# The last output projection of an RWKV layer: operands loaded ahead, the last window results split in place, and the next stage's first weights in turn with it

## The chip, the cores and the metric

The kernel runs on one core of a Trainium2 chip. The metric is the device time of one execution in microseconds (us), the median of several runs. The engines are named as in the profile: PE (TensorE matmul) and PEld (its weight load), DVE (VectorE), ACT (ScalarE), POOL (GpSimd) and SP (SyncE, which here only issues transfers). ACT and POOL have DMA queues of their own too.

## The reference

One inference step of a two-layer trunk, over 1024 prompt tokens and 8 x 16 sample tokens, 1024 features wide, in float32:

```python
# layer 0
r, k, v, decay, a_gate, g = projections(h, h_prev)
y, wkv_new = wkv7_scan(r, decay, k, v, -kk, kk * a_gate, wkv_prev)
y = ((y - mu) * lax.rsqrt(var + LNX_EPS)).reshape(bsz, t, d)      # per head of 64
y = y * ln_w + ln_b
y = y + bonus                                                     # (r k r_k) summed over a head, times v
out = (y * g) @ w_o
x = x + gt_m[:, None, :] * out
h = modulate(rms_norm(x, norm_ffn), sh_f, sc_f)
x = x + gt_f[:, None, :] * swiglu(h, w_gate, w_up, w_down)
# layer 1: shared K/V, chunk-band attention, then another SwiGLU FFN
```

`rms_norm` divides by the root of the mean square over the 1024 features of a token; `modulate` scales and shifts by per-request vectors.

## The kernel before, in words

Everything lies with features on the 128 partitions (8 feature tiles, f = 0 to 7) and tokens in the columns. The 1152 tokens are three blocks b of 384; in the last one columns 0 to 255 are prompt tokens and 256 to 383 sample tokens. A float32 product is made in three TensorE passes: each operand x is split (`split`, L267 to L269) into a rounded part, copied by ACT (L268), and the rest, subtracted by DVE (L269), and `mm3` (L271) multiplies high by high, high by low and low by high.

**The windows.** Layer 0's recurrence runs over windows of 128 tokens: nine windows w, each in two halves hf of four feature tiles. `windows` (L1115) runs them in pairs. The last six halves come in the order (6,0) (6,1) (8,0) (7,0) (7,1) (8,1), where w = 8 holds the samples. A half ends with TensorE's group Y (64x64 matmuls), then with `win_post` (L1046 to L1071): ACT copies Y to a tile y (L1056), TensorE centers it, ACT squares it (L1059), TensorE sums the squares per head, ACT takes logarithm and exponential (L1063, L1064), DVE multiplies by the centered value (L1065), applies weight and bonus bv (four L1069) and the gate gl (L1070), and ACT's queue stores the tile to yg in DRAM (L1071). The tiles y, bv and gl exist once each (`self.wt(tag, ..., 1)`); the ring "TT" has six tiles of the same size and serves steps earlier in a window.

**The output projection.** `outproj(b)` (L1158 to L1182) loads its eight operand tiles mr from yg (L1166, on SP), splits them into mx tiles, then makes one unit for each output tile f: `wunit` (L258) loads the weights into one of two raw tiles (L256; the queue is POOL's here, `self.wqueue`) and splits them into whi and wlo, of which there are two each; 24 matmuls of 128x384 go into one of two acc banks; `residual` (L1148) adds the gate times the product to x, loaded as rr: L1151 for the prompt columns, L1155 and L1156 for the samples; the sum e is stored to x1 in DRAM (L1179, on SP), and its squares are added up (L306 on ACT, L307 on DVE). Behind the last unit `sq_done` (L309) sums over the partitions on TensorE (bank aux) and `rsqrt2` makes the norm factors r (L326 to L330), which are stored to rr in DRAM (L1182). outproj(0) and outproj(1) run in turn with the last six halves (`early`); outproj(2) comes after them. A unit's 24 matmuls are ordered k = 0 to 7 over the operand tiles.

**The FFN's start.** `dense` forms the FFN's gate and up products in a one-level Strassen scheme. Its tokens are two column groups: group 0 is columns 0 to 511, group 1 columns 512 to 1151, of which 256 prompt columns and the 128 samples come from block 2. For each group, `part` (L1436) loads the norm factors from rr (L1438), and `strassen_in` (L1255) loads eight x tiles from x1 (L1262), scales them (`normed`: L349 on DVE, L350 on ACT; for samples L357 to L359 on DVE), and forms combinations on POOL (L1268: twelve for a group of tiles with two inputs, four that only negate or copy) whose splits are the h tiles. `strassen_weights` (L1291) loads weight quarters rq (L1304) and splits them and their sums (L1309 to L1312, here on DVE) into w tiles. `gate_up` (L1319) then makes, for each of 22 steps and each group, seven products of 24 matmuls in banks S and PT, added on DVE and POOL (L1338) and stored (L1359).

The code names the order of the parts, but the framework places each instruction on its engine by a schedule of its own, so that parts which don't depend on each other interleave. On an engine instructions run strictly in the order placed: one that waits holds all behind it. A DMA issue waits in the same way on its queue.

Of the kernel before, what the change touches and what calls it, by code (L numbers as in the profile page):

```python
# [141 lines left out]
class Trunk:  # L142
# [166 lines left out]
    def sq_done(self, st):  # L309
# [9 lines left out]
        r = self.ev("rms", 1)[:, :w]  # L319
        self.rsqrt2(r, ss, self.ev("kk", 2)[:, :w], 1024, 0)  # L320
        return r
# [724 lines left out]
    def win_post(self, w, hf, R):  # L1046
# [4 lines left out]
        gt = self.wt("gl", [128, 512], 1)  # L1051
        nc.sync.dma_start(gt.rearrange("p (f t) -> p f t", f=4), self.sp[b]["g"][:, wi, fs, :])
        bv = self.wt("bv", [128, 512], 1)
        nc.sync.dma_start(bv.rearrange("p (f t) -> p f t", f=4), self.sp[b]["v"][:, wi, fs, :])
        y = self.wt("y", [128, 512], 1)
# [15 lines left out]
        nc.scalar.dma_start(self.yg[b][:, fs, wi * 128:(wi + 1) * 128], y.rearrange("p (f t) -> p f t", f=4))  # L1071
# [85 lines left out]

    def outproj(self, b):  # L1158

        nc, pp = self.nc, self.pp  # L1160
        cols = slice(b * TB, (b + 1) * TB)
        hi, lo = [], []
        for f in range(8):
            h, l = self.mtile(), self.mtile()
            t = self.mraw()
            nc.sync.dma_start(t, self.yg[b][:, f, :])  # L1166
            self.split(h, l, t)
            hi.append(h)
            lo.append(l)
# [12 lines left out]
        nc.sync.dma_start(self.rr[:, cols], self.sq_done(st))  # L1182

    def layer0a(self, ctx):
        self.yg = [self.dp.tile([128, 8, TB], F32, name=f"yg{b}") for b in range(NB)]
# [16 lines left out]
        def early():  # L1202
            yield from self.alternate(self.outproj(0), self.ada, 1, 1)
            yield from self.outproj(1)
        for _ in self.alternate(self.windows([divmod(int(x), 2) for x in '12 13 16 14 15 17'.split()]), early(), 1, 2):
            pass
        cw.close()
        for _ in self.outproj(2):
            pass
        self.wqueue = None  # L1210
# [5 lines left out]
    def wide_open(self, ctx, name):  # L1216
        self.wq = ctx.enter_context(self.tc.tile_pool(name="wq" + name, bufs=1, reuse_waits="tile"))
        self.rawtag = "h0"
        self.hw = ("w", "w", 16)
        self.halfraw = lambda: self.wq.tile([128, 512], F32, tag="rq", name=self.nm("rq"), bufs=5)  # L1220

# [201 lines left out]
    def dense(self, x2, x3, close):  # L1423
# [4 lines left out]
        with ExitStack() as ctx:  # L1428
            pool = lambda n, **k: ctx.enter_context(self.tc.tile_pool(name=n, bufs=1, reuse_waits="tile", **k))
            self.hps = {0: pool("h0")}  # L1430
            with ExitStack() as c2:
                self.wide_open(c2, "0")
# [15 lines left out]

                for _ in part(0, lambda: self.wq.tile([128, 512], F32, tag="w", name=self.nm("x"), bufs=16)):
                    pass  # L1450
                W = list(self.strassen_weights(0, 0, nc.vector))
# [501 lines left out]
```

## Time and profile before

| | us |
|---|---|
| median of 3 runs | 3858.28 (3854.87 to 3863.27) |
| the profiled execution's own time | 3864.46 |
| its span, first to last instruction | 3862.7 |
| mean granted TensorE clock | 0.932 |
| PE busy, of the span | 3540.6 (92%) |
| DVE / ACT / POOL busy | 2291.8 / 1575.7 / 643.2 |

The profile's page divides the span into 40 equal slices with each engine's busy share. The stage that the change touches, from the last halves to the start of the FFN, lies at about 1190 to 1400 us of the span; the rest are the earlier projections, the FFN of layer 0, the attention and its FFN. A row of a timeline is: start, duration, engine, line, operation, output<-input, shapes, count, and in brackets the idle time of the engine before it with what ended that. "PE clock" is the share of the full TensorE clock that was granted.

### The profile page before, as it was taken

The numbers are of one execution on the slowest core, as the hardware profiler recorded it, in microseconds if no ns is written. First come the engines' busy times: TensorE is split into PE (matmuls) and PEld (weight loads), VectorE is DVE, ScalarE is ACT, GpSimd is POOL, SyncE is SP. The second block draws the span as 40 slices with busy tenths as digits, with TensorE's granted clock in tenths as the row PEclk, the third lists the DMA queues.
The fourth block names the chain that finished last, engine by engine and source line by source line (L and its number), as shares of the span: only waits on it lengthen the run. The fifth ranks groups of instructions, "written<-read, shape, count | busy, mean of one in ns | idle before, by whom it ended". The sixth has DMA issues, their size and how long they took to land.

```text
span 3862.7 us, 72343 instructions
## 1 busy us (share of the span) xinstructions
PE 3540.6 (92%) x28614; PEld 3125.0 (81%) x28614; DVE 2291.8 (59%) x4420; ACT 1575.7 (41%) x2998; POOL 643.2 (17%) x564
## 2 busy tenths in 40 slices
PE   5889989989888699999999899789889799999999
PEld 4777778777666599999887879677777799999998
DVE  4666666765445764554456752666675764554567
ACT  5545646544223433333311353565654533333310
POOL 0000000000010364453000100000000254453000
PEclk8887998889798789999999999899999899999999
DMA  5775776776664412223755112454555322222521
GB/s 209 233 218 163 214 207 182 200 199 199 187 201 147 143 67 75 74 75 105 254 179 182 70 62 97 141 152 140 153 185 167 116 80 75 74 75 92 171 86 70
DMA packets 428963, 552.31 MB, mean 143 GB/s; under 512 B 128432, under 2 KB 296880, under 8 KB 424144
## 3 DMA queue, kind: packets, MB, share of 16 engines
q1 hardware_dynamic: 352640, 449.49, 36.4%
q0 software_dynamic: 21840, 79.31, 6.8%
q10 hardware_dynamic: 54144, 18.89, 2.1%
q8 instruction: 225, 3.69, 0.4%
q14 instruction: 114, 0.93, 0.1%
HBM read 413.42 MB, written 134.12 MB: 142 GB/s over the span
## 4 chain that ended last, share of the span: by engine, by line
PE 69%; DMA 9%; DVE 9%; issue 6%; ACT 5%; POOL 1%; SPq 1%; ACTq 0%; DVEq 0%; POOLq 0%
PE S L139 31%; PE PT L139 15%; PE acc L139 13%; PE st L139 3%; PE O L139 2%; PE G L139 1%; DVE h L269 1%; PE PT L1779 1%; PE aux L139 1%; DMA raw<-in_wada 1%; DMA TT<-Z 1%; DMA Z<-T 1%; DVE wlo L269 1%; PE Y L139 1%; ACT pts L1780 1%
## 5 line engine op out<-in xcount | busy, mean ns | idle before, releaser
L139 PE MATMUL S<-h,w 128*128 128x320 f32 (+1 forms) x4944 | 698.9, 300 | 18.2 <-DVE h L269 7.7
L139 PEld LDWEIGHTS S<-h,w 128*128 128x128 f32 x4944 | 676.8, 192 | 26.6 <-DVE h L269 12.8
L139 PE MATMUL acc<-mx,whi 128*128 128x384 f32 x1728 | 512.5, 374 | 41.8 <-ACT mx L268 20.2
L139 PE MATMUL S<-h,wh 128*128 128x320 f32 (+1 forms) x2844 | 529.8, 337 | 14.0 <-DVE h L1151 8.1
L139 PEld LDWEIGHTS S<-h,wh 128*128 128x128 f32 x2844 | 455.4, 189 | 70.6 <-issue 11.7
L139 PEld LDWEIGHTS acc<-mx,whi 128*128 128x128 f32 x1728 | 340.4, 205 | 74.1 <-ACT mx L268 23.9
L268 ACT ACTIVATE w<-rq 128x512 fp32r<-128x512 f32 x308 | 192.4, 629 | 503.5 <-PE S L139 203.1
L269 DVE TENSOR_TENSOR w<-rq,w 128x512 fp32r<-128x512 f32 x308 | 268.6, 875 | 199.5 <-ACT w L268 198.9
L139 PE MATMUL PT<-h,w 128*128 128x320 f32 (+1 forms) x2448 | 355.4, 300 | 14.1 <-ACT w L268 6.9
L139 PEld LDWEIGHTS PT<-h,w 128*128 128x128 f32 x2448 | 337.9, 192 | 17.8 <-ACT w L268 7.1
L139 PE MATMUL acc<-mx,wlo 128*128 128x384 f32 x864 | 318.8, 369 | 6.5 <-DVE wlo L269 6.5
L139 PE MATMUL PT<-h,wh 128*128 128x320 f32 (+1 forms) x1428 | 286.4, 344 | 10.8 <-DVE wh L269 3.9
L1338 POOL TENSOR_TENSOR t<-t,t 128x576 f32<-128x576 f32 (+1 forms) x132 | 216.5, 1641 | 417.0 <-ACT t L1345 295.3
L139 PEld LDWEIGHTS PT<-h,wh 128*128 128x128 f32 x1428 | 233.5, 190 | 41.7 <-issue 6.0
L269 DVE TENSOR_TENSOR wlo<-raw,whi 128x1024 fp32r<-128x1024 f32 x114 | 139.6, 1226 | 85.3 <-ACT whi L268 84.3
L139 PEld LDWEIGHTS acc<-mx,wlo 128*128 128x128 f32 x864 | 176.7, 205 | 16.3 <-DVE wlo L269 10.3
L269 DVE TENSOR_TENSOR h<-h,h 128x1024 fp32r<-128x1024 f32 (+4 forms) x112 | 122.9, 1111 | 89.9 <-ACT h L268 73.0
L268 ACT ACTIVATE wh<-rq 128x512 fp32r<-128x512 f32 x124 | 74.8, 625 | 242.8 <-PE S L139 160.7
L268 ACT ACTIVATE h<-h 128x1024 fp32r<-128x1024 f32 (+4 forms) x112 | 103.3, 935 | 168.1 <-DMA h<-sd 111.7
L268 ACT ACTIVATE whi<-raw 128x1024 fp32r<-128x1024 f32 x114 | 119.6, 1053 | 124.3 <-PE acc L139 78.9
L1338 DVE TENSOR_TENSOR t<-S,t 128x576 f32<-128x576 f32 (+1 forms) x116 | 86.4, 745 | 132.0 <-PE S L139 132.0
L1405 DVE TENSOR_TENSOR h<-h,S 128x640 f32<-128x640 f32 (+1 forms) x150 | 111.9, 750 | 78.8 <-PE S L139 78.7
(433 smaller groups left out, 5754.7 us busy)
## 6 DMA issues: line engine op xcount, KB each, us to landing
h<-in_wada SPq DMA_DIRECT2D x64, 512.0 KB, 6.4
rq<-in_wg SPq DMA_DIRECT2D x88, 256.0 KB, 2.6
rq<-in_wu SPq DMA_DIRECT2D x88, 256.0 KB, 2.6
rq<-in_wd SPq DMA_DIRECT2D x88, 256.0 KB, 3.0
raw<-in_wada POOLq DMA_DIRECT2D x32, 512.0 KB, 5.0
kc<-in_ck SPq DMA_DIRECT2D x16, 1024.0 KB, 5.0
vc<-in_cv SPq DMA_DIRECT2D x16, 1024.0 KB, 5.8
sd<-t SPq DMA_DIRECT2D x88, 160.0 KB, 1.9
```

The costliest lines, as they stand in the source:

```text
L139: return nc.tensor.matmul(out, lhsT, rhs, start=start, stop=stop)
L268: self.nc.scalar.activation(hi, x, AF.Copy)
L269: self.nc.vector.tensor_tensor(lo, x, hi, ALU.subtract)
L1338: eng.tensor_tensor(out, x, y, ALU.add)
L1405: nc.vector.tensor_tensor(y, y, d, ALU.add)
L1779: nc.tensor.transpose(pt[:, j * 128:(j + 1) * 128], P[:, j * 128:(j + 1) * 128], self.C("ident"))
L1780: nc.scalar.activation(pts[:, 0:nk * 128], pt[:, 0:nk * 128], AF.Copy)
```

## The change

1. `win_post` for half (7,1) takes three tiles of the ring "TT" for gl, bv and y, in place of the single tiles.
2. For halves (7,1) and (8,1) the result isn't stored to yg. It is split at once into the four operand tiles f = 4 to 7 of the last output projection (`last_in()`), columns wi * 128 on.
3. `last_in` makes these operands once, at the end of `early`: f = 0 to 3 are loaded whole from yg, f = 4 to 7 only for their first 128 columns, with `self.wload`, which is POOL's queue here.
4. `outproj(2)` is moved out of `layer0a` into `dense`, behind group 0's `part(0)`, in turn with the first weight quarters: four steps of it to one of theirs. To that end `wide_open` is divided in two.
5. For b = 2 the norm factors aren't stored to rr but kept in a tile `self.r2`; group 1 loads 256 columns of rr and copies the other 384 from r2 on ACT.

```diff
 win_post:
-        gt = self.wt("gl", [128, 512], 1)
+        new = lambda tag: self.wt(tag, [128, 512], 1)
+        if (w, hf) == (7, 1):
+            new = lambda tag: self.wt("TT", [128, 8, 64], 6).rearrange("p c t -> p (c t)")
+        gt = new("gl")
...
-        nc.scalar.dma_start(self.yg[b][:, fs, wi * 128:(wi + 1) * 128], ...)
+        if hf == 1 and w > 6:
+            cs = slice(wi * 128, (wi + 1) * 128)
+            for f in range(4):
+                h, l = (t[4 + f][:, cs] for t in self.last_in())
+                self.split(h, l, y[:, f * 128:(f + 1) * 128])
+        else:
+            nc.scalar.dma_start(self.yg[b][:, fs, wi * 128:(wi + 1) * 128], ...)
+    def last_in(self):
+        if not self.yin:
+            self.yin = self.out_in(2, self.wload, 128)
+        return self.yin
 outproj, its operands in a function of their own:
+    def out_in(self, b, load, n=TB):
+        hi, lo = [], []
+        for f in range(8):
+            h, l = self.mtile(), self.mtile()
+            m = TB if f < 4 else n
+            t = self.mraw()[:, :m]
+            load(t, self.yg[b][:, f, :m])
+            self.split(h[:, :m], l[:, :m], t)
...
+        hi, lo = self.last_in() if b == 2 else self.out_in(b, nc.sync.dma_start)
...
-        nc.sync.dma_start(self.rr[:, cols], self.sq_done(st))
+        if b < 2:
+            nc.sync.dma_start(self.rr[:, cols], self.sq_done(st))
+        else:
+            self.r2 = self.halfraw()[:, :TB]
+            self.sq_done(st, self.r2)
 layer0a:
             yield from self.outproj(1)
+            self.last_in()
...
-        for _ in self.outproj(2):
-            pass
 dense, part(c):
-                    nc.sync.dma_start(r, self.rr[:, self.cols(c)])
+                    if c:
+                        nc.sync.dma_start(r[:, 0:256], self.rr[:, 512:768])
+                        nc.scalar.activation(r[:, 256:640], self.r2, AF.Copy)
+                    else:
+                        nc.sync.dma_start(r, self.rr[:, self.cols(c)])
...
-                W = list(self.strassen_weights(0, 0, nc.vector))
+                for _ in self.alternate(self.outproj(2), weights(), 4, 1):
+                    pass
```

In the pieces of the order below, line numbers of the kernel before are those of the profile; in the changed kernel the lines of `win_post` are 3 higher, those of `residual` 15, those of the FFN's start 27. A name's number tells one tile from another.

ACT at the end of the windows, before. y_13379 is the result of half (7,1), y_13491 that of (8,1), mr and mx the operands of outproj(2):

```order
L1056 ACTIVATE y_13379<-Y_13341 128x512
L1059 ACTIVATE y_13379<-st_13381 128x512
L1063 ACTIVATE y_13379<-st_13394,eps 128x512
L1064 ACTIVATE y_13379<-y_13379 128x512
L1071 DMA yg_114<-y_13379 128x4x128
L1056 ACTIVATE y_13491<-Y_13405 128x512
L1059 ACTIVATE y_13491<-st_13493 128x512
L1063 ACTIVATE y_13491<-st_13496,eps 128x512
L1064 ACTIVATE y_13491<-y_13491 128x512
L1071 DMA yg_114<-y_13491 128x4x128
L268 ACTIVATE mx_13532<-mr_13534 128x384
L268 ACTIVATE mx_13538<-mr_13540 128x384
```

The same place of ACT after, where TT_13379 is the result of (7,1) and y_13546 that of (8,1) (the copy of Y is now L1059, the square L1062, Ln and Exp L1066 and L1067):

```order
L1059 ACTIVATE TT_13379<-Y_13341 128x512
L268 ACTIVATE mx_13430<-mr_13432 128x128
L268 ACTIVATE mx_13436<-mr_13438 128x128
L1062 ACTIVATE TT_13379<-st_13381 128x512
L1066 ACTIVATE TT_13379<-st_13442,eps 128x512
L1067 ACTIVATE TT_13379<-TT_13379 128x512
L1059 ACTIVATE y_13546<-Y_13460 128x512
L268 ACTIVATE mx_13418<-TT_13379 128x128
L268 ACTIVATE mx_13424<-TT_13379 128x128
L268 ACTIVATE mx_13430<-TT_13379 128x128
L268 ACTIVATE mx_13436<-TT_13379 128x128
L1062 ACTIVATE y_13546<-st_13548 128x512
```

Both stores are gone, and the splits of a result stand where its store was, the four of (7,1) behind the copy of (8,1) and ahead of its square. The loads' splits stand earlier, some between the steps of (7,1).

DVE around the first residual of outproj(2), before. x are group 0's tiles being scaled, h their splits, e the output of the residual of f = 0:

```order
L349 SCALAR_TENSOR_TENSOR x_13908<-x_13908,mod,x_13903 128x512
L349 SCALAR_TENSOR_TENSOR x_13909<-x_13909,mod,x_13903 128x512
L269 TENSOR_TENSOR h_13914<-x_13906,h_13913 128x256
L269 TENSOR_TENSOR mx_13551<-mr_13552,mx_13550 128x384
L349 SCALAR_TENSOR_TENSOR x_13910<-x_13910,mod,x_13903 128x512
L269 TENSOR_TENSOR h_13914<-x_13907,h_13913 128x256
L349 SCALAR_TENSOR_TENSOR x_13911<-x_13911,mod,x_13903 128x512
L269 TENSOR_TENSOR h_13916<-x_13908,h_13915 128x256
L1151 SCALAR_TENSOR_TENSOR e_2356_13589<-acc_13562,mod,rr_13587 128x256
L1155 TENSOR_TENSOR e_2356_13589<-acc_13562,mod 128x128
```

The same place after, where the x tiles are numbered 13581 to 13588:

```order
L269 TENSOR_TENSOR mx_13437<-y_13546,mx_13436 128x128
L349 SCALAR_TENSOR_TENSOR x_13581<-x_13581,mod,x_13580 128x512
L349 SCALAR_TENSOR_TENSOR x_13582<-x_13582,mod,x_13580 128x512
L349 SCALAR_TENSOR_TENSOR x_13583<-x_13583,mod,x_13580 128x512
L1166 SCALAR_TENSOR_TENSOR e_2379_13733<-acc_13706,mod,rr_13731 128x256
L349 SCALAR_TENSOR_TENSOR x_13584<-x_13584,mod,x_13580 128x512
L1170 TENSOR_TENSOR e_2379_13733<-acc_13706,mod 128x128
L1166 SCALAR_TENSOR_TENSOR e_2392_13785<-acc_13746,mod,rr_13783 128x256
L1170 TENSOR_TENSOR e_2392_13785<-acc_13746,mod 128x128
L269 TENSOR_TENSOR h_13591<-x_13581,h_13590 128x256
L349 SCALAR_TENSOR_TENSOR x_13585<-x_13585,mod,x_13580 128x512
L1171 TENSOR_TENSOR e_2379_13733<-e_2379_13733,rr_13731 128x128
```

Before, all eight L349 stand ahead of the first residual; after, three do, and the other five are mixed with what follows it.

POOL's queue through outproj(2), before. raw are the weights of the units; the first four are those of f = 0 to 3:

```order
L256 DMA raw_13637<-in_rw_o 128x1024
L256 DMA raw_13678<-in_rw_o 128x1024
L1268 ISA
L1268 TENSOR_TENSOR x_13908<-x_13908,x_13904 128x256
L1268 TENSOR_TENSOR x_13904<-x_13904 128x256
L1268 TENSOR_TENSOR x_13904<-x_13904,x_13908 128x256
L256 DMA raw_13719<-in_rw_o 128x1024
L1268 TENSOR_TENSOR x_13909<-x_13909,x_13905 128x256
L1268 TENSOR_TENSOR x_13908<-x_13908,x_13904 128x256
L256 DMA raw_13760<-in_rw_o 128x1024
```

The same place after, where raw_13793 is that of f = 2, raw_13888 of f = 4 and raw_13929 of f = 5:

```order
L256 DMA mr_13408<-yg_114 128x384
L256 DMA mr_13414<-yg_114 128x384
L256 DMA mr_13420<-yg_114 128x128
L256 DMA mr_13426<-yg_114 128x128
L256 DMA mr_13432<-yg_114 128x128
L256 DMA mr_13438<-yg_114 128x128
L256 DMA raw_13888<-in_rw_o 128x1024
L256 DMA raw_13929<-in_rw_o 128x1024
L1295 ISA
L1295 TENSOR_TENSOR x_13585<-x_13585,x_13581 128x256
L1295 TENSOR_TENSOR x_13581<-x_13581 128x256
L1295 TENSOR_TENSOR x_13581<-x_13581,x_13585 128x256
```

The operand loads mr stand in POOL's queue ahead of the weights of f = 4; the weights of f = 4 and 5 stand ahead of all combinations. Those of f = 6 and 7 (raw_13974, raw_14019) follow behind the ninth and the twelfth combination, where before they followed behind the fifteenth and the sixteenth.

More of the change, by code (lines that the diff above doesn't have):

```diff
@@ L307, in sq_add, with sq_done @@
             (nc.gpsimd if gp else nc.vector).tensor_tensor(st.acc, st.acc, t, ALU.add)
-    def sq_done(self, st):
+    def sq_done(self, st, r=None):
         w = st.acc.shape[-1]
@@ L318, in sq_done @@
             mm(self.nc, z, self.C("ones"), st.acc[:, o:o + n], True, True)
-        r = self.ev("rms", 1)[:, :w]
+        r = self.ev("rms", 1)[:, :w] if r is None else r
         self.rsqrt2(r, ss, self.ev("kk", 2)[:, :w], 1024, 0)
@@ L1050, in win_post @@
         fs = slice(4 * hf, 4 * hf + 4)
-        gt = self.wt("gl", [128, 512], 1)
+        new = lambda tag: self.wt(tag, [128, 512], 1)
+        if (w, hf) == (7, 1):
+            new = lambda tag: self.wt("TT", [128, 8, 64], 6).rearrange("p c t -> p (c t)")
+        gt = new("gl")
         nc.sync.dma_start(gt.rearrange("p (f t) -> p f t", f=4), self.sp[b]["g"][:, wi, fs, :])
-        bv = self.wt("bv", [128, 512], 1)
+        bv = new("bv")
         nc.sync.dma_start(bv.rearrange("p (f t) -> p f t", f=4), self.sp[b]["v"][:, wi, fs, :])
-        y = self.wt("y", [128, 512], 1)
+        y = new("y")
         nc.scalar.activation(y, R.Y, AF.Copy)
@@ L1070, in win_post @@
         nc.vector.tensor_tensor(y, y, gt, ALU.mult)
-        nc.scalar.dma_start(self.yg[b][:, fs, wi * 128:(wi + 1) * 128], y.rearrange("p (f t) -> p f t", f=4))
+        if hf == 1 and w > 6:
[4 more added lines that the diff above has]
+        else:
+            nc.scalar.dma_start(self.yg[b][:, fs, wi * 128:(wi + 1) * 128], y.rearrange("p (f t) -> p f t", f=4))
+    def last_in(self):
+        if not self.yin:
+            self.yin = self.out_in(2, self.wload, 128)
+        return self.yin
     @staticmethod
@@ L1156, in residual @@
             nc.vector.tensor_tensor(out[:, n:], t, x[:, n:], ALU.add)
+    def out_in(self, b, load, n=TB):
[6 more added lines that the diff above has]
+            self.split(h[:, :m], l[:, :m], t)
+            hi.append(h)
+            lo.append(l)
+        return hi, lo
     def outproj(self, b):
@@ L1161, in outproj @@
         cols = slice(b * TB, (b + 1) * TB)
[L1162 to L1169, printed above, removed]
+        hi, lo = self.last_in() if b == 2 else self.out_in(b, nc.sync.dma_start)
         st = self.sq_open()
@@ L1181, in outproj @@
             yield
-        nc.sync.dma_start(self.rr[:, cols], self.sq_done(st))
+        if b < 2:
[3 more added lines that the diff above has]
+            self.sq_done(st, self.r2)
     def layer0a(self, ctx):
+        self.yin = None
         self.yg = [self.dp.tile([128, 8, TB], F32, name=f"yg{b}") for b in range(NB)]
@@ L1207, in layer0a, with wq_open, wide_open @@
         cw.close()
-        for _ in self.outproj(2):
-            pass
-        self.wqueue = None
         ct.push(c1)
         return ct.close
-    def wide_open(self, ctx, name):
+    def wq_open(self, ctx, name):
         self.wq = ctx.enter_context(self.tc.tile_pool(name="wq" + name, bufs=1, reuse_waits="tile"))
-        self.rawtag = "h0"
         self.hw = ("w", "w", 16)
         self.halfraw = lambda: self.wq.tile([128, 512], F32, tag="rq", name=self.nm("rq"), bufs=5)
+    def wide_open(self, ctx, name):
+        self.wq_open(ctx, name)
+        self.rawtag = "h0"
     def wide_open2(self, ctx, name):
@@ L1431, in dense @@
             with ExitStack() as c2:
-                self.wide_open(c2, "0")
+                self.wq_open(c2, "0")
                 A = self.gain("nf0", 32)
@@ L1447, in done, with weights @@
                     yield from self.normed_split(c, *X[c], self.Ak, 96, *HK[c])
+                W = []
+                def weights():
+                    for t in self.strassen_weights(0, 0, nc.vector):
+                        W.append(t)
+                        yield
                 for _ in part(0, lambda: self.wq.tile([128, 512], F32, tag="w", name=self.nm("x"), bufs=16)):
                     pass
-                W = list(self.strassen_weights(0, 0, nc.vector))
+                for _ in self.alternate(self.outproj(2), weights(), 4, 1):
+                    pass
+                self.wqueue = None
+                self.rawtag = "h0"
                 close()
```

## The prediction

> **What bounds the kernel now.** I read the page first: a span of 3862.7 us, 1.8 less than the profiled execution's own 3864.46, which is 6.2 above the median of 3858.28. The change touches one stage, so I cut it into slices (columns: busy time and count of PE, PEld, DVE, ACT, POOL; PE clock; DMA share; GB/s).
>
> ```profile
> span 3862.7 us, 72343 instructions
> ```
>
> ```profile
> core 0: us, PE busy (x) PEld busy (x) DVE busy (x) ACT busy (x) POOL busy (x), PEclk, DMA share, GB/s
> 1220.00:1240.00 20.00, 20.00 (x277) 13.57 (x275) 8.92 (x24) 3.13 (x6) 0.00 (x0) 1.00 0.15 50
> 1240.00:1260.00 20.00, 4.27 (x7) 1.02 (x5) 5.04 (x12) 2.79 (x5) 0.00 (x0) 0.56 0.17 53
> 1260.00:1280.00 20.00, 11.97 (x35) 9.55 (x36) 15.74 (x31) 13.68 (x28) 3.80 (x1) 0.67 0.66 223
> 1280.00:1300.00 20.00, 12.71 (x52) 11.91 (x52) 17.90 (x26) 10.14 (x23) 18.25 (x19) 0.76 0.33 105
> 1300.00:1320.00 20.00, 16.37 (x87) 14.81 (x85) 15.12 (x33) 6.98 (x12) 0.57 (x1) 0.99 0.39 127
> 1320.00:1340.00 20.00, 15.51 (x91) 14.55 (x91) 10.65 (x27) 10.19 (x20) 2.00 (x2) 0.77 0.47 159
> 1340.00:1360.00 20.00, 14.86 (x46) 11.70 (x45) 19.38 (x36) 10.56 (x24) 14.49 (x12) 0.50 0.21 66
> 1380.00:1400.00 20.00, 20.00 (x152) 20.00 (x152) 11.64 (x14) 6.19 (x11) 13.17 (x10) 1.00 0.26 89
> ```
>
> TensorE is full and at full clock on both sides of 1240 to 1380, and neither in between. In 1240 to 1260 no engine is busy: a chain of single steps. From 1260 DVE is the fullest (15.7 and 17.9 of 20), and again at 1340 (19.4). So three limits follow one another: latency, DVE's work, and group 1's splits on DVE.
>
> The first, in ACT's timeline and below it PE's:
>
> ```profile
> 1242.94 0.43 ACTq L1071 DMA_DIRECT2D yg<-y  x1
> 1247.06 0.60 ACT L1056 ACTIVATE y<-Y 128x512 f32<-128x512 f32 x1 [6.78 <-DMA yg<-y]
> 1249.82 0.60 ACT L1059 ACTIVATE y<-st 128x512 f32<-128x512 f32 x1 [2.16 <-PE st L139]
> 1256.59 0.37 ACTq L1071 DMA_DIRECT2D yg<-y  x1
> 1261.39 1.02 ACT L268 ACTIVATE mx<-mr 128x384 fp32r<-128x384 f32 x2 [7.46 <-DMA mr<-yg]
> 1267.09 0.40 ACT L268 ACTIVATE h<-x 128x256 fp32r<-128x256 f32 x1
> ```
>
> ```profile
> 1238.83 1.30 PE L139 MATMUL Y<-XL,ssv 64*64 64x16 f32 x30
> 1247.71 2.07 PE L139 MATMUL st<-y,cst 128*128 128x512 f32 x2 [7.59 <-ACT y L1056]
> 1261.97 1.33 PE L139 MATMUL acc<-mx,whi 128*128 128x384 f32 x3 [9.42 <-ACT mx L268]
> 1269.00 1.28 PE L139 MATMUL acc<-mx,whi 128*128 128x384 f32 x3 [2.82 <-ACT mx L268]
> 1272.85 0.38 PE L139 MATMUL acc<-mx,wlo 128*128 128x384 f32 x1
> ```
>
> Y of (8,1) is done at 1240.13 (first row of PE), but its copy runs at 1247.06, since the only tile y is still being stored for (7,1). Its own store at 1256.59 must land and be loaded again before PE goes on at 1261.97, and the operand tiles come two by two, a second wait of 2.82.
>
> **The change part by part.** All is counted against the profiled execution.
>
> *Own tiles for (7,1).* The copy of (8,1) no longer waits for the store: it can start at 1240.3. Its square now stands behind the four splits of (7,1), which wait for the last product of (7,1) on DVE:
>
> ```profile
> 1242.22 0.69 DVE L1070 TENSOR_TENSOR y<-y,gl 128x512 f32<-128x512 f32 x1
> 1255.87 0.69 DVE L1070 TENSOR_TENSOR y<-y,gl 128x512 f32<-128x512 f32 x1
> 1266.72 1.42 DVE L349 SCALAR_TENSOR_TENSOR x<-x,mod,x 128x512 f32<-128x512 f32 x2 [0.29 <-DMA x<-x]
> 1280.85 1.42 DVE L269 TENSOR_TENSOR h<-x,h 128x256 fp32r<-128x256 f32 x4
> ```
>
> That product ends at 1242.91. A split of 384 columns costs 0.51 on ACT (1.02 for two), one of 256 up to 0.40; for 128 I take 0.23, so four are 0.9. The square starts at about 1243.9, not 1249.82: 5.9 saved (6.8 less 0.9). If a split cost the whole 0.40 it would be 5.2.
>
> *Split in place.* Before, 5.41 passed from DVE's end (1256.56) to PE's start (1261.97): store, load, split. Now one ACT copy and one DVE subtraction of 128 columns: about 0.7. Saved: 4.7. The wait of 2.82 for the second pair goes with it, as all tiles of k = 4 to 7 come from one result: 2.8. So the last products of units 0 and 1 end 13.4 earlier, at 1259.8 in place of 1273.23.
>
> *What DVE gives back.* Before, by that time DVE had scaled all eight x tiles of group 0 and subtracted five h parts; after, only three L349 stand ahead of the first residual in its order, and since instructions run in order DVE waits there although the x tiles, now loaded ahead, are ready. Five L349 at 0.67 (1.42 for two overlapping) and five splits at 0.33 (1.42 for four) come behind: 5.0 more. That is owed in full only where DVE bounds what follows:
>
> ```profile
> 1273.58:1317.28 43.70, 31.70 (x144) 29.15 (x144) 38.88 (x71) 20.93 (x42) 22.62 (x20) 0.84 0.34 107
> ```
>
> DVE is busy 38.9 of the 43.7 from the first residual to the last. I take +5.0; 0 if the 4.8 of slack absorbed it, and no more than 5.0 as no other work is added.
>
> *POOL's queue.* Here lies the largest stall of that stretch, unit 4's:
>
> ```profile
> 1293.49 0.98 PE L139 MATMUL acc<-mx,whi 128*128 128x384 f32 x2 [5.22 <-DVE e L1155]
> 1296.53 0.69 PE L139 MATMUL acc<-mx,wlo 128*128 128x384 f32 x1 [2.06 <-DVE wlo L269]
> ```
>
> ```profile
> 1276.20 6.66 POOL L1268 TENSOR_TENSOR x<-x,x 128x256 f32<-128x256 f32 x1 [63.53 <-DVE h L269]
> 1284.44 0.58 POOL L256 DMA_DIRECT2D raw<-in_rw_o  x1
> 1292.44 4.63 POOL L1268 TENSOR_TENSOR x<-x,x 128x256 f32<-128x256 f32 x4
> 1297.02 0.57 POOL L256 DMA_DIRECT2D raw<-in_rw_o  x1
> 1302.59 0.57 POOL L256 DMA_DIRECT2D raw<-in_rw_o  x1 [4.12 <-DVE wlo L269]
> ```
>
> The weights of unit 4 were issued at 1284.44, behind a combination of 6.66; now they and unit 5's stand ahead of all combinations, and the stall of 5.2 + 2.1 goes. But the weights of units 6 and 7 stand behind nine and twelve combinations, which now begin late, behind the issue for unit 5, that waits for a split on DVE. So the next stall is unit 6's. I take 0 for the exchange, from −3 to +3.
>
> What a combination costs decides here: four took 4.63 (1.16 each), the first 6.66, while DVE ran without a break until 1282.3. The Trainium skill, "SBUF — State Buffer", section "SBUF: two separate sides", gives a rule: a DVE instruction with two SBUF inputs and a POOL one that reads SBUF share a port pair, an exclusive lock that either holds for its whole instruction. The row of 6.66 agrees. By the rule alone, a DVE kept full would hold up each combination, and the exchange would cost some 20 (the rival below); by the row of 4.63 it costs 0.
>
> *Operand loads on POOL's queue.* Eight loads move from SP to POOL; those that matter are long before the end of the windows.
>
> ```profile
> raw<-in_rw_o POOLq DMA_DIRECT2D x7, 512.0 KB, 3.9
> mr<-yg SPq DMA_DIRECT2D x8, 192.0 KB, 3.1
> ```
>
> POOL's larger loads land in 3.9, SP's in 3.1. They are hidden behind the windows, whose Y fills PE to 1240; but their splits stand in ACT's and DVE's rows ahead of steps of (7,1), which wait if a load is late. I put +1, from 0 to +4. On SP the x loads of group 0 no longer stand behind the mr loads: counted above.
>
> *Norm factors kept.* Before, group 1's first step waits through sum, store, load of rr and then loads of x:
>
> ```profile
> 1316.99 0.29 DVE L1156 TENSOR_TENSOR e<-e,rr 128x128 f32<-128x128 f32 x1
> 1321.81 0.56 DVE L330 SCALAR_TENSOR_TENSOR rms<-kk,rms 128x384 f32<-128x384 f32 x1
> 1329.69 0.29 DVE L357 TENSOR_TENSOR x<-x,x 128x128 f32<-128x128 f32 x1 [7.32 <-DMA x<-x]
> ```
>
> From the last residual's end (1317.28) to L357 it is 12.4. Now the x loads follow the last x1 store at once, beside the factor's 5.1 (to 1322.37), and an ACT copy of 384 columns, 0.5, follows: 5.8 with a small gap. Saved: 6.6, and PE gets it, because DVE is full with these tiles at 1340 to 1360 while PE runs at half clock. Bounds: −7, if the copy is free; −2, if the x loads land late or other DVE work takes the place. What would be late next is again group 1's splits.
>
> *Elsewhere* instructions of PE, DVE and ACT change places in the earlier windows and the attention, without work added; 0, from −3 to +3.
>
> Sum: −5.9 − 4.7 − 2.8 + 5.0 + 0 + 1 − 6.6 + 0 = −14.0. From the execution's 3864.46 that is 3850.5; from the median, 3858.3 − 14.0 = **3844.3**, forecast as 3844.
>
> **The rivals.**
>
> *Slower: POOL held up behind DVE.* At 1273 to 1317 DVE is 89% busy, and nearly all its work has two SBUF inputs. If its runs are now unbroken, a combination costs more; the next price that the trace shows for such an operation is 2.73:
>
> ```profile
> 1343.02 2.73 POOL L1338 TENSOR_TENSOR rq<-rq,rq 128x256 f32<-128x256 f32 x1 [4.10 <-DVE rq L1338]
> ```
>
> Sixteen combinations at 2.73 in place of about 1.1 last 26 longer; twelve of them stand ahead of unit 7's weights, which come 20 later. With unit 7 late by that, and group 0's splits (the h tiles of b12, b11, b22, b21) too, −14 turns to +6: 3864. It decides from about 2.3 a combination, where the twelve cost the 14. For it: 6.66 in the first. Against it: in the slice 1280 to 1300 nineteen POOL instructions took 18.25, 1 each, the tail of the 6.66 among them, with DVE 17.9 of 20 busy. Chance 0.07. (The rule of the Trainium skill's page "SBUF — State Buffer", section "SBUF: two separate sides", would make this case the likely one; the trace agrees in one combination out of sixteen.)
>
> *About the same: DVE is the bound and takes it back.* If DVE's 38.9 us simply follow the start and the 5.0 are joined by stalls for units 6 and 7 (+3), late operand splits (+4), and the factors give only 2 since group 1's splits are bound by DVE's total, it is −13.4 + 5 + 3 + 4 − 2 = −3.4, 3855; between that and −7.7, no change can be told. For it: the DVE figures of 1280 and 1340. Against: DVE is idle 7.32 ahead of L357, so that time is there to take. Chance 0.17.
>
> *More: the residual's stalls go too.* If the 5.0 are absorbed in the slack and the stall of 7.3 goes without one in its place, it is −14 − 5 − 7.3 = −26, 3832. For it: x tiles loaded ahead, weights of units 4 and 5 too. Against: DVE's order. Chance 0.16.
>
> The change does what it says, in the order shown: no store of (7,1), (8,1) or the factors is left, so that rival is none.
>
> **How the numbers follow.** 0.60 for the forecast, with its own range of −8 to −20; 0.16, 0.17 and 0.07 for the rivals. Two thousandths of 3858 are 7.7 us, about what a measurement here can tell from no change. Faster by more than that: 0.60 + 0.16 = 0.76; same 0.17; slower 0.07. The range takes in the larger gain and most of the small one: 3831 to 3855, which leaves out the slower case, half of the small gain and some 0.05 at the lower end, about 0.2.
>
> **What would show it.** In the changed profile: the copy of Y of (8,1) at once behind Y, no wait for a store; PE's acc at about 1251 without the waits of 9.42 and 2.82; DVE waiting at the first residual, then full; PE stalled ahead of unit 6, not unit 4, by up to 5; combinations of about 1 us on POOL; the last residual 7 to 11 earlier than 1317; group 1's first L357 about 6 behind it, not 12.4. It is wrong if POOL's combinations cost over 2 us, if PE's stalls up to 1380 grow by what was gained ahead of them, or if the windows ahead of 1240 end later because an operand load holds ACT or DVE.

## The result, and the profile after

The changed kernel took 3845.43 us (median of 9 runs; 3863.47 for the kernel before beside it). One of the nine ran at a granted clock of 0.309 and took 10688.57; the ratio is formed without it. The ratio is 0.9943, with an interval of 0.9928 to 0.9958: by it the change is 22 us faster (16 to 28). The forecast was 14 faster, 3844 as against a median of 3858.28. That 3845 lies so near 3844 is luck: the kernel before took 5 us more in this series than in the one that the forecast started from. Two more series of the changed kernel, told below, gave 0.9936 (0.9921 to 0.9950) and 0.9945 (0.9926 to 0.9964). The direction and the places were forecast; the size was short by some 8 us.

The profiled execution took 3845.66 with a span of 3843.7, 19.0 less than before. Its slices, with the columns of those shown of before:

```profile
1240.00:1260.00 20.00, 11.37 (x37) 8.86 (x38) 11.88 (x29) 11.04 (x25) 0.53 (x1) 0.67 0.49 164
1260.00:1280.00 20.00, 16.96 (x87) 16.32 (x85) 19.17 (x34) 10.93 (x25) 14.30 (x12) 0.92 0.31 93
1280.00:1300.00 20.00, 10.93 (x48) 10.34 (x48) 18.12 (x33) 9.09 (x18) 5.42 (x8) 0.74 0.36 122
1340.00:1360.00 20.00, 18.71 (x108) 17.34 (x108) 16.46 (x22) 7.56 (x16) 10.86 (x10) 0.78 0.16 53
1360.00:1380.00 20.00, 20.00 (x153) 20.00 (x152) 10.09 (x15) 6.74 (x12) 10.21 (x8) 1.00 0.32 101
```

The empty slice behind 1240 is half filled, and TensorE is full from 1360 on, where before it still stood at 16.96 of 20 from 1360 to 1380. What remains is the dip at 1280 to 1300, with DVE at 18 to 19 of 20 ahead of it and in it.

ACT's timeline, where the waits for the store (6.78) and the load (7.46) stood:

```profile
1237.59 0.60 ACT L1059 ACTIVATE y<-Y 128x512 f32<-128x512 f32 x1 [0.25 <-PE Y L139]
1239.99 0.91 ACT L268 ACTIVATE mx<-TT 128x128 fp32r<-128x128 f32 x4 [1.81 <-DVE TT L1073]
1240.81 0.57 ACT L1062 ACTIVATE y<-st 128x512 f32<-128x512 f32 x1
1247.55 0.91 ACT L268 ACTIVATE mx<-y 128x128 fp32r<-128x128 f32 x4 [2.66 <-DVE y L1073]
```

The copy runs at once behind Y. The four splits of (7,1) take 0.91 and the square stands right behind them, as in the order. Then TensorE's timeline:

```profile
1235.88 1.68 PE L139 MATMUL Y<-XL,ssv 64*64 64x16 f32 x40
...
1247.91 1.33 PE L139 MATMUL acc<-mx,whi 128*128 128x384 f32 x3 [4.40 <-ACT mx L268]
1252.24 0.84 PE L139 MATMUL acc<-mx,whi 128*128 128x384 f32 x2
1253.17 0.52 PE L139 MATMUL acc<-mx,whi 128*128 128x384 f32 x2
1254.40 0.34 PE L139 MATMUL acc<-mx,wlo 128*128 128x384 f32 x1
1287.14 0.98 PE L139 MATMUL acc<-mx,whi 128*128 128x384 f32 x2 [7.82 <-ACT w L268]
1290.05 0.69 PE L139 MATMUL acc<-mx,wlo 128*128 128x384 f32 x1 [1.94 <-DVE wlo L269]
```

Y ends at 1237.56, units 0 and 1 at 1254.74; from 1253.17 on two matmuls take 0.52, not 0.84. The stall of 5.22 + 2.06 ahead of unit 4 is gone; one of 7.82 + 1.94 stands ahead of unit 6. DVE's timeline at the end of the projection:

```profile
1300.97 0.29 DVE L1171 TENSOR_TENSOR e<-e,rr 128x128 f32<-128x128 f32 x1
1306.93 0.29 DVE L357 TENSOR_TENSOR x<-x,x 128x128 f32<-128x128 f32 x1 [0.59 <-ACT x L1467]
```

Group 1 starts 5.67 behind the last residual (1301.26), not 12.41.

**A measure for the stage.** Spans of one kernel scatter, as will be seen, by more than an edit is worth. So I count TensorE's matmuls in the 200 us from the end of Y of (8,1). All kernels below come to full clock inside that time, where 152 matmuls are made in 20 us (the row of 1380:1400 of before), 7.6 in one. The difference of the counts, divided by 7.6, is by how much the stage is ahead. First before, then the changed kernel (PE's count in brackets):

```profile
1240.15:1440.15 200.00, 152.67 (x839) 138.15 (x840) 130.68 (x217) 82.36 (x159) 84.74 (x67) 0.80 0.31 102
```

```profile
1237.59:1437.59 200.00, 164.08 (x1002) 153.66 (x1003) 139.37 (x234) 88.82 (x175) 90.50 (x74) 0.86 0.29 97
```

(1002 − 839) / 7.6 = 21.4 us ahead: the whole measured gain of 22 lies in this stage. The lead can be had in a second way, as TensorE makes the same 17318 matmuls behind Y in every kernel here, so that the Nth of one can be set beside the Nth of another. The 400th comes 21.7 us earlier than before the change, the 5000th, some 770 us behind Y, 22.1 earlier, and the last one 16.6. So nothing is gained in the later part of the program; what changes there is scatter, as the next section shows. The kernel before has a single profile: an error in its count would shift all leads below alike.

### The profile page after: what moved, and what is told of

The parts are those of the page before. It is cut to its first block, busy times and chain, and to the rows that moved or that the text cites. A ratio compares the mean times of both kernels' runs of the same rounds, so it can differ in the third digit from the quotient of the medians.

```text
span 3843.7 us, 72360 instructions
## 1 busy us (share of the span) xinstructions
PE 3531.3 (92%) x28614; PEld 3121.7 (81%) x28614; DVE 2297.0 (60%) x4428; ACT 1575.3 (41%) x3007; POOL 645.9 (17%) x572
## 4 chain that ended last, share of the span: by engine, by line
PE 70%; DMA 10%; DVE 9%; issue 4%; ACT 4%; SPq 1%; POOL 1%; ACTq 0%; DVEq 0%; POOLq 0%
PE S L139 32%; PE PT L139 15%; PE acc L139 12%; PE st L139 3%; PE O L139 2%; DVE h L269 1%; PE G L139 1%; PE PT L1819 1%; PE aux L139 1%; PE Y L139 1%; DMA TT<-Z 1%; DMA raw<-in_rw_o 1%; DVE wlo L269 1%; DMA Z<-T 1%; DMA h<-qT 1%
## 5 line engine op out<-in xcount | busy, mean ns | idle before, releaser
L139 PEld LDWEIGHTS PT<-h,w 128*128 128x128 f32 x2448 | 336.1, 191 | 12.5 <-ACT w L268 4.2
L139 PE MATMUL PT<-h,wh 128*128 128x320 f32 (+1 forms) x1428 | 287.2, 344 | 10.5 <-DVE wh L269 3.9
```

The source lines that it names most:

```text
L139: return nc.tensor.matmul(out, lhsT, rhs, start=start, stop=stop)
```

## The experiments

My theory after the result: the gain is the sum of a shorter chain (own tiles; no store and load) and of the kept factors, and what is left ahead of unit 6 comes from POOL's queue. Rivals: that DVE bounds the stage and gives a part back; that the new turn of projection and weights is what gained; and that the later half of the program moved.

### The changed kernel again, twice

No edit. The first stood beside three of the kernels below, the second beside the last.

> The changed kernel once more, beside the next three on one chip. Its stage, from the end of Y of half (8,1) to TensorE full again, was 115.1 us in its first profile and 137.0 before; if these lengths belong to the kernels and not to single executions, it is 113 to 117 again, with the stall ahead of unit 6 at 6 to 8 us. The ratio is 0.993 to 0.997.

> The changed kernel a third time, beside the next run. The matmuls that TensorE makes in the 200 us from the end of Y of half (8,1) were 839 before the change and 1002 and 1014 in two executions of the changed kernel, and 7.6 are made in a microsecond at full clock; so a stage that belongs to the kernel gives 1000 to 1016 again, while the span may differ by 10 us or more. Ratio 0.992 to 0.996.

Ratios 0.9936 and 0.9945, both as expected, and so were the stall ahead of unit 6 in the first (6.25) and the count of the second. The spans of the profiled executions were 3829.4 and 3849.5, that of the first 3843.7. The counts, one row of each:

```profile
1231.78:1431.78 200.00, 166.66 (x1014) 155.49 (x1015) 139.93 (x235) 88.90 (x175) 92.14 (x75) 0.86 0.29 97
```

```profile
1241.35:1441.35 200.00, 165.98 (x1012) 154.90 (x1013) 139.03 (x234) 88.88 (x175) 91.86 (x74) 0.87 0.30 97
```

The stage is 21.4, 23.0 and 22.8 us ahead: it repeats within 1.6 us, while the span differs by 20. About half of that had already come by the end of Y, which lies just ahead of each row's start: 1231.75 in the one, 1241.32 in the other. Much of the rest comes behind the stage: the leads over the kernel before are 23.8 and 23.0 us at the 5000th matmul, 25.1 and 14.5 at the last. So the stage's count can tell 2 to 3 us, the times of whole runs some 6 to 9 (half the width of an interval).

### Factors through DRAM again

```diff
-        if b < 2:
-            nc.sync.dma_start(self.rr[:, cols], self.sq_done(st))
-        else:
-            self.r2 = self.halfraw()[:, :TB]
-            self.sq_done(st, self.r2)
+        nc.sync.dma_start(self.rr[:, cols], self.sq_done(st))
...
-                    if c:
...
+                    nc.sync.dma_start(r, self.rr[:, self.cols(c)])
```

> The changed kernel with its fifth part undone: the norm factors of block 2 go through DRAM again (store to rr, then group 1 loads all 640 columns); all else as changed. If the chain behind the last residual sets the start of group 1 (the term of 6.6 in the sum), the first L357 comes 12.4 us behind the last residual's end, not the 5.7 of the changed kernel, TensorE is full again 6 to 7 us later, and the ratio to the kernel before is about 0.996. Rival: DVE's total work for group 1 bounds the stage whenever it starts, and the early start only lengthens waits: then L357 is late too, but TensorE is full at most 2 us later.

Ratio 0.9959 (0.9944 to 0.9974). DVE's last residual and the first L357, and the count:

```profile
1294.35 0.29 DVE L1171 TENSOR_TENSOR e<-e,rr 128x128 f32<-128x128 f32 x1
1307.18 0.29 DVE L357 TENSOR_TENSOR x<-x,x 128x128 f32<-128x128 f32 x1 [1.91 <-DMA x<-x]
```

```profile
1230.84:1430.84 200.00, 164.71 (x943) 151.60 (x944) 137.71 (x229) 86.27 (x169) 88.97 (x71) 0.82 0.29 95
```

L357 comes 12.5 behind the residual, and the stage is 13.7 ahead of before, 7.7 to 9.3 less than the changed kernel. The factors are worth their whole 6.7 and a little more; the rival's 2 is out.

### Single tiles for (7,1) again

```diff
-        if (w, hf) == (7, 1):
-            new = lambda tag: self.wt("TT", [128, 8, 64], 6).rearrange("p c t -> p (c t)")
```

> The changed kernel with own tiles for half (7,1) undone: it takes the single gl, bv and y again, but its result is still split in place. The store that held y before (6.8 us) is gone all the same, so if the wait for the store was what mattered, the copy of Y of (8,1) waits only for the splits of (7,1), about 3.6 us later than in the changed kernel, and TensorE starts the operand tiles f = 4 to 7 about 3.5 us later; the stage ends 2 to 4 us later. Rival: the own tiles buy nothing, as the splits of (7,1) stand ahead of the square of (8,1) anyway: 0 to 1 us later.

Ratio 0.9972 (0.9958 to 0.9985). ACT's copy of (8,1), and the count:

```profile
1252.12 0.60 ACT L1057 ACTIVATE y<-Y 128x512 f32<-128x512 f32 x1 [0.42 <-DVE mx L269]
```

```profile
1249.22:1449.22 200.00, 162.52 (x969) 149.45 (x970) 136.94 (x230) 87.13 (x173) 89.25 (x72) 0.86 0.31 100
```

The copy waits for the splits of (7,1), 2.9 behind the end of Y (1249.19) where it was 0.03. The stage is 17.1 ahead: 4.3 to 5.9 lost. So the tiles are worth about 5 even without the store, a little more than the 2 to 4 I expected.

### Results stored and loaded again

```diff
-        if hf == 1 and w > 6:
+        if False:
...
-            self.last_in()
...
-            self.yin = self.out_in(2, self.wload, 128)
+            self.yin = self.out_in(2, self.nc.sync.dma_start)
```

> The changed kernel with both results stored to yg and all eight operand tiles loaded whole on SP, as before (own tiles for (7,1) kept). By the sum of the prediction, the store, load and split take 4.7 us more and the second pair of operands 2.8 more, so units 0 and 1 end about 7.5 us later after the end of Y. Since group 0's x tiles are loaded ahead and their combinations now stand ahead of the weights of unit 4, DVE and POOL can work in that gap: if DVE's work bounds what follows, up to 5 us come back before the last residual. Theory of the chain: last residual 6 to 8 us later than in the changed kernel. Rival (DVE bound): 0 to 3 us later.

Ratio 0.9971 (0.9956 to 0.9986). TensorE's resumption, DVE's last residual, and the count:

```profile
1259.57 1.33 PE L139 MATMUL acc<-mx,whi 128*128 128x384 f32 x3 [12.06 <-ACT mx L268]
```

```profile
1310.46 0.29 DVE L1171 TENSOR_TENSOR e<-e,rr 128x128 f32<-128x128 f32 x1
```

```profile
1242.45:1442.45 200.00, 158.53 (x958) 146.25 (x959) 137.62 (x226) 87.06 (x169) 84.47 (x72) 0.83 0.31 101
```

TensorE waits 12.06, against 4.40. The last residual ends 68.3 behind Y (1242.41), 4.6 to 6.0 later than in the changed kernel: less than the 6 to 8 expected, more than the 0 to 3 of the rival. The stage is 15.7 ahead, 5.7 to 7.3 lost, so the chain's share is real, and DVE took a small part of it back.

The three losses (8.7, 5.3 and 6.7 against the mean of 22.4) add up to 20.7 of 22.4: within what the count can tell, the three edits' gains add, and together they are nearly the whole.

### Order of the code as before

```diff
-                for _ in part(0, ...):
-                    pass
-                for _ in self.alternate(self.outproj(2), weights(), 4, 1):
-                    pass
-                self.wqueue = None
+                for _ in self.outproj(2):
+                    pass
+                self.wqueue = None
+                for _ in part(0, ...):
+                    pass
+                for _ in weights():
+                    pass
```

> The changed kernel with the code's order of its fourth part undone: outproj(2), then part(0), then the first weights, not in turn. The placed order on POOL stays nearly the same (weights of units 4 and 5 ahead of the combinations, 6 behind eight and 7 behind eleven), so if the gain comes from the operands, the store and the factors, the time is that of the changed kernel within 3 us. Rival: the turn of outproj(2) and the weights is where the gain comes from; then it is 8 us or more slower.

Ratio 0.9958 (0.9942 to 0.9975). The count:

```profile
1244.38:1444.38 200.00, 164.59 (x1008) 153.88 (x1009) 137.47 (x234) 88.50 (x175) 87.79 (x74) 0.87 0.30 98
```

22.2 ahead, the same: the code's order, the projection in turn with the weights, is not where the gain comes from. Its last residual came 58.2 us behind the end of Y, in place of 62.3 to 63.7, but group 1 gave that back, the first such case.

### Operands on SP's queue

```diff
-            self.yin = self.out_in(2, self.wload, 128)
+            self.yin = self.out_in(2, self.nc.sync.dma_start, 128)
```

> The changed kernel with the operands of the last output projection loaded on SP's queue, not POOL's. The prediction put the loads on POOL at +1 us (0 to 4). If they cost that, the steps of (7,1) and so the copy of Y come up to 4 us earlier against the end of Y; if they are hidden behind the windows, nothing changes within 2 us. As the combinations then stand nearer to the front of POOL's queue, unit 6 stands behind seven of them in place of nine and its stall may be 1 to 2 us shorter.

Ratio 0.9950 (0.9937 to 0.9963). The count:

```profile
1228.98:1428.98 200.00, 164.27 (x1005) 152.97 (x1006) 139.85 (x234) 89.24 (x176) 90.66 (x74) 0.86 0.29 97
```

21.8 ahead: the queue of these loads costs nothing that shows. The stall ahead of unit 6 was not shorter (8.88), so that guess missed.

### Weights of units 6 and 7 on SP's queue

```diff
         for f in range(8):
+            if b == 2 and f > 5:
+                self.wqueue = None
             W = self.wunit(pp, self.a["rw_o"][f])
```

> The changed kernel with the weights of units 6 and 7 loaded on SP's queue, so that they no longer stand behind nine and twelve of POOL's combinations. If POOL's queue is what makes unit 6 late, its weights are issued about 8 us earlier, as soon as unit 4's are split, the stall of 7.8 and the 1.9 behind it go, and the last residual comes 5 to 8 us earlier. Rival: DVE, busy 43.5 of the 46.5 us from the first residual to the last, bounds this stretch; then at most 3 us are gained and the stall only moves to another unit.

Ratio 0.9938 (0.9916 to 0.9960), beside 0.9936 of the changed kernel. In the changed kernel POOL issued unit 6's weights at

```profile
1278.83 0.57 POOL L256 DMA_DIRECT2D raw<-in_rw_o  x1
```

which is 23.3 behind the first residual (its L1170 starts at 1255.49). Here SP issues them; its row, TensorE's row of unit 6, and the count:

```profile
1266.49 0.33 SPq L256 DMA_DIRECT2D raw<-in_rw_o  x1
```

```profile
1281.87 0.98 PE L139 MATMUL acc<-mx,whi 128*128 128x384 f32 x2 [5.47 <-DVE e L1170]
```

```profile
1234.36:1434.36 200.00, 168.48 (x1021) 157.25 (x1022) 139.49 (x235) 89.36 (x176) 92.33 (x73) 0.86 0.30 97
```

The weights go out 15.4 behind the first residual (1251.05 here), 8 earlier, as expected, and still TensorE stands for 5.47, now for a residual on DVE. The last residual comes 61.0 behind Y, 1.3 to 2.7 sooner, and the stage is 23.9 ahead. My cause for this stall, POOL's queue, falls: it was only the last wait of several. The rival holds: DVE is late, and at most 3 us are gained.

### Group 0's combinations on DVE

```diff
 strassen_in:
-        gp = nc.gpsimd
+        gp = nc.vector if c == 0 else nc.gpsimd
```

> The changed kernel with group 0's sixteen combinations on DVE in place of POOL; POOL's queue then holds nothing between the weights of units 4 and 7. DVE gets 16 instructions of about 0.33, 5.3 us more. In the changed kernel, while POOL combines (1266 to 1286), sixteen splits on DVE take 12.0 us in place of 5.3, and others about 1.8 more, as if POOL's instructions held DVE up. Theory of the shared access: DVE loses 8 in order to spare 5, so without POOL the last residual comes 3 to 9 us earlier, the weights' wait included. Rival: DVE is bound by its own work, and those long splits only waited for data; then the last residual comes 2 to 5 us later.

Ratio 0.9907 (0.9883 to 0.9930). DVE's splits of 128x256 in the stretch 1250 to 1305 (count | busy, mean ns), in the changed kernel and here:

```profile
L269 DVE TENSOR_TENSOR h<-x,h 128x256 fp32r<-128x256 f32 x28 | 16.7, 633 | 0.5 <-ACT h L268 0.5
```

```profile
L269 DVE TENSOR_TENSOR h<-x,h 128x256 fp32r<-128x256 f32 x28 | 10.5, 411 | 0.0
...
L1295 DVE TENSOR_TENSOR x<-x,x 128x256 f32<-128x256 f32 x12 | 4.9, 410 | 0.0
L1295 DVE TENSOR_TENSOR x<-x 128x256 f32<-128x256 f32 x4 | 1.6, 412 | 0.0
```

```profile
1237.21:1437.21 200.00, 167.83 (x1020) 156.85 (x1021) 140.33 (x251) 88.70 (x176) 76.22 (x59) 0.87 0.29 97
```

Without POOL beside them the same 28 splits take 10.5 us, not 16.7: POOL's combinations had held them up by 6.2, about as much as the sixteen cost DVE itself (4.9 for the twelve with two inputs, 1.6 for the other four). Against the rival, that the long splits only waited for data, speaks the changed kernel itself: of its 28 splits the 13 that no POOL instruction overlaps took 410 to 420 ns; of the 15 others seven took the same, six 941 to 976, one 611 and one 3081. The stall of 7.8 ahead of unit 6 is gone, and the last residual comes 59.0 behind Y, 3.3 to 4.7 sooner. That is the theory's sign and the lower half of its size. But the stage is only 23.8 ahead, 0.8 to 2.4 more than the changed kernel: group 1 gives most of it back.

The ratio is better by some 11 us, more than the stage can account for. The edit reaches further than I meant: the second FFN forms its operands in the same `strassen_in`, so its combinations moved too. They lie between the 11500th and the 12500th matmul, and there the lead over the kernel before grows by 8.9 us, where in the nine executions of this document with all combinations on POOL it changes by −0.5 to 2.4. The intervals of the two ratios still overlap, so by whole runs alone this gain isn't shown.

### All combinations on DVE

```diff
-        gp = nc.gpsimd
+        gp = nc.vector
```

> The changed kernel with all combinations of the operands of both FFNs on DVE, those of group 1 too (the run before moved only group 0's). In group 1's stretch, from the first L357 to TensorE full again (45.5 us), 28 splits of 128x320 on DVE take 23.6 us, 0.88 each, where the ones without a POOL instruction beside them take about 0.40 at intervals (0.48 each at the start of the stretch). If POOL holds DVE up there as well, the splits fall to 0.5 each, DVE gains some 10 and pays 16 combinations of about 0.4, 6.4: the stretch gets 3 to 8 us shorter, and the kernel 0.1 to 0.2% faster than with group 0's alone, 0.989 to 0.990 of the kernel before. Rival: DVE is bound by its own work here; the stretch gets 4 to 6 us longer.

Ratio 0.9912 (0.9891 to 0.9932). Group 1's splits in the stretch 1290 to 1350, in the second series of the changed kernel and here, the longest wait of TensorE here, then the wait of ACT and the POOL instruction that led to it, and the count:

```profile
L269 DVE TENSOR_TENSOR h<-x,h 128x320 fp32r<-128x320 f32 x28 | 23.6, 875 | 1.0 <-ACT h L268 1.0
```

```profile
L269 DVE TENSOR_TENSOR h<-x,h 128x320 fp32r<-128x320 f32 x28 | 13.4, 498 | 0.1
```

```profile
1344.33 1.17 PE L139 MATMUL S<-h,w 128*128 128x320 f32 x3 [9.04 <-ACT t L1372]
```

```profile
1342.44 0.63 ACT L268 ACTIVATE w<-rq 128x512 fp32r<-128x512 f32 x1 [9.83 <-POOL rq L1339]
```

```profile
1330.21 8.18 POOL L1336 TENSOR_TENSOR rq<-rq,rq 128x512 f32<-128x512 f32 x1 [9.57 <-DMA rq<-in_wu]
```

```profile
1239.04:1439.04 200.00, 161.58 (x1020) 153.42 (x1021) 135.65 (x267) 88.97 (x176) 66.55 (x43) 0.90 0.31 97
```

The splits fall from 0.875 to 0.498 us, as foreseen, but TensorE's stretch isn't shorter: a wait of 9.04 for ACT takes the place of the many small ones, and the stage is 23.8 ahead as in the run before. Neither my 3 to 8 us nor the rival's loss came. The rows say why. A POOL addition of weight quarters took 8.18, where the same one took 1.52 in the changed kernel; DVE ran combinations and splits without a break until 1337.27, and the addition ended 1.1 behind that. ACT's next weight split waits for the third addition after it, and ACT's t stands behind that split. So here POOL was held up behind DVE, and by these waits it cost TensorE the 9. The second FFN gains again, 10.5 between the same two matmuls.

### The same with the weights of units 6 and 7 on SP's queue and the order as before

```diff
+            if b == 2 and f > 5:
+                self.wqueue = None
...
-                for _ in self.alternate(self.outproj(2), weights(), 4, 1):
+                for _ in self.outproj(2):
```

> The same with the weights of units 6 and 7 on SP's queue and the code's order of outproj(2), part(0) and the weights as before the change. Each of the two shortened the stretch from the end of Y to the last residual by 1 to 5 us in the changed kernel (60.96 and 58.24 in place of 62.3 to 63.7). If the stalls they remove are still there when POOL no longer combines, it is 1 to 5 us faster than the run beside it; if the run beside it has already lost them, as the stalls ahead of unit 6 were 1.1 and 1.9 with group 0's combinations on DVE, it is the same within 2 us.

Ratio 0.9931 (0.9913 to 0.9950). The count:

```profile
1245.43:1445.43 200.00, 167.43 (x1042) 158.84 (x1043) 137.26 (x270) 89.18 (x177) 65.27 (x43) 0.88 0.31 99
```

26.7 ahead, 2.9 more than the run beside it, as the first of the two cases expected; the whole runs do not show it (0.9931 and 0.9912 overlap). In the second FFN it gains 10.0.

### The three edits of the projection's stretch together

Group 0's combinations on DVE, weights of units 6 and 7 on SP's queue, the order of the code as before; the edits are those shown above.

> The changed kernel with three edits together: group 0's combinations on DVE (group 1's stay on POOL), the weights of units 6 and 7 on SP's queue, and the code's order of outproj(2), part(0) and the weights as before the change. With all combinations on DVE the same order made 1042 matmuls in the 200 us from the end of Y, 3 us more than the changed kernel's best. If that comes from the stretch up to the last residual, where all three edits lie, this run makes 1030 to 1045 too; rival: the group-1 combinations were what gained, and it makes 1010 to 1025.

Ratio 0.9925 (0.9906 to 0.9943), beside 0.9945 of the changed kernel. DVE's last residual and first L357, and the count:

```profile
1291.82 0.29 DVE L1171 TENSOR_TENSOR e<-e,rr 128x128 f32<-128x128 f32 x1
...
1300.06 0.29 DVE L357 TENSOR_TENSOR x<-x,x 128x128 f32<-128x128 f32 x1 [0.34 <-DMA x<-x]
```

```profile
1240.92:1440.92 200.00, 171.27 (x1036) 158.81 (x1037) 140.71 (x253) 88.92 (x176) 74.66 (x58) 0.87 0.30 99
```

Behind the end of Y (1240.89) the last residual comes at 51.2, 11 to 12.5 us sooner than in the changed kernel, and no wait of TensorE up to there is over 1.3 once it has resumed. The count, 1036, is as expected of the stretch up to the last residual. But the stage is 25.9 ahead, only 2.9 to 4.5 more than the changed kernel. Some 8 us are given back behind the last residual: L357 follows it by 7.95 in place of 5.67, and the rest goes in group 1's stretch, where its cause stays open. By the stage's count this version and the one before it (26.7) are level; in the second FFN it gains 5.9. By whole runs it isn't told apart from the changed kernel.

## Why the prediction was right, point by point

The terms, against the two first profiles (from the end of Y):

| step | forecast | measured |
|---|---|---|
| end of Y to TensorE's return (own tiles, split in place) | −10.6 | 21.84 to 10.35: −11.5 |
| return to the end of units 0 and 1 | −2.8 | 11.26 to 6.83: −4.4 |
| end of units 0 and 1 to the last residual (DVE's backlog, POOL's queue) | +5.0 | 44.05 to 46.52: +2.5 |
| last residual to the first L357 (factors) | −6.6 | 12.41 to 5.67: −6.7 |
| operand loads on POOL | +1 | nothing seen (own experiment: 21.8 beside 21.4 to 23.0) |
| group 1 up to full clock | 0 | −1.3 (the rest of the 21.4) |
| sum | −14.0 | −21.4 |

**Own tiles and split in place: right.** The square, forecast behind the four splits, is there, and the splits' 0.9 was 0.91. Undoing the two edits cost 5.3 and 6.7, against terms of 5.9 and 7.5.

**Units 0 and 1: mis-sized.** I took the wait of 2.82 away and left the rest as it was. But TensorE now ran without a break from 1247.91, and its granted clock, 0.51 up to 1253.17, was 1.00 from there on, so the last eight of the 24 matmuls went at full rate (two in 0.52, not 0.84). That is most of the 1.6 more; in the other two executions it was 2.5 and 2.7.

**DVE's backlog: there in full, but not owed in full.** From the first residual to the last the changed kernel has

```profile
1254.43:1301.26 46.83, 30.88 (x146) 28.51 (x144) 43.84 (x80) 25.59 (x53) 20.25 (x20) 0.85 0.31 100
```

DVE's busy time there rose from 38.88 (of 43.70) to 43.84 (of 46.83), the 5.0 of the forecast, and its idle time fell from 4.8 to 3.0: a part went into the slack. The +5.0 was the upper end of its own range; with the exchange of stalls, put at 0, it came to 2.5 here and to 2.0 and 3.4 in the other two executions.

**POOL's queue: the place was right, the cause wrong.** The stall moved from unit 4 to unit 6 as the order showed, and was 7.82, not up to 5. I laid it to POOL's queue; with the weights issued 8 us earlier, 5.47 of it was left. DVE comes late to the residual, and POOL's combinations are a large part of that: 633 ns a split beside them, 411 without. But they were so before the change too, as the view of the same 28 splits in the stretch 1250 to 1310 shows:

```profile
L269 DVE TENSOR_TENSOR h<-x,h 128x256 fp32r<-128x256 f32 x28 | 15.3, 574 | 2.0 <-ACT h L268 1.9
```

From 15.3 to 16.7 is 1.4. So POOL's hold on DVE was there in both kernels, and makes little of the difference between them.

**Factors: right**, 6.7 for 6.6, and PE got it: undone, 8.7 was lost.

**Operand loads: nothing to be seen**, not +1.

So the errors in size all lie on one side, 7.4 us together, and none of the four steps had the wrong sign. By the difference of 22 the gain lies outside the forecast's own −8 to −20; the whole range held it because it reached to the rival with the larger gain.

**The rival on the slower side** had POOL held up behind DVE. It didn't come: the changed kernel's combinations, by POOL's view of the tile (min/median/max in ns), took

```profile
L1295 POOL TENSOR_TENSOR x<-x,x x12: 716/922/1716, 1266.1 to 1284.4; 128x256 f32<-128x256 f32 x12
L1295 POOL TENSOR_TENSOR x<-x x4: 724/920/4126, 1267.6 to 1280.1; 128x256 f32<-128x256 f32 x4
```

with one of sixteen over 2 us. But DVE paid too, 6.2 us over its 28 splits, and I had priced the shared access for POOL alone. (The Trainium skill, "SBUF — State Buffer", section "SBUF: two separate sides", says that the loser blocks fully, whichever it is; the 633 and 411 ns agree that DVE can be the one.) Where DVE ran without a break, POOL paid: 4.13 once in the changed kernel, and 8.18 with all combinations on DVE. **DVE takes it back**, the rival with no change, is half true: not for the change as made, whose parts add up, but for most of the further gains ahead of the last residual. Of the 12 us of the three edits together 8 were given back; of the 2 that the weights on SP's queue brought, most stayed.

## What to carry to other kernels

In a stretch where one engine after the other is the limit, price a chain's shortening by what the next stretch can use: the change's own gains came through whole, but a further 12 us ahead of the last residual left only some 4 at the stage's end. Where two engines share an access, price both sides: moving work to an idle engine cost the busy one about as much here as the work itself. Where an edit goes into a function that serves two places, look at both. And where whole runs scatter by more than an edit is worth, measure progress of the bounding engine over a fixed time behind a common event.

## What the runs showed of the hardware that was not expected

- POOL's tensor operations beside DVE's two-input ones lengthened DVE's from 411 to 633 ns (128x256) and from 498 to 875 ns (128x320), on the mean over 28 each; POOL's own median was 0.92 us. With no combination left on POOL, the 128x256 ones took 0.41 on DVE.
- One POOL operation beside an unbroken run of DVE took 6.66 us before the change, one 4.13 after, and one 8.18 with all combinations on DVE, where others of the kind took 0.72 to 1.72; in the last case it ended 1.1 us behind that run.
- Three profiled executions of one and the same kernel differ by 20 us in span (3829.4 to 3849.5) at a mean granted clock of 0.933 to 0.938, though one stage repeats within 1.6 us.
